# Another start for a one-core layer kernel: the input is turned and scaled by products with diagonals, the first adaLN block is loaded ahead of it, and its sums go to VectorE

## The chip, the cores and the metric

One core of one Trainium2 chip runs the whole program. The metric is the device time of one execution in microseconds. The kernel before has a median of 2390.36 us over three runs (2387.80, 2390.36 and 2390.41 us). About 0.2% (some 4.8 us) is what a measurement of this kernel can tell from no change.

## What is computed

One layer: an adaLN norm, one large projection, a gated convolution beside a chunked gated delta rule, an output projection, a gated feed-forward part and a final adaLN norm. The change touches only the first lines of it.

```python
def adaln(x, gain, shift, scale):
    return rms_norm(x, gain) * (1 + scale[:, None, :]) + shift[:, None, :]
...
    c_act = jax.nn.silu(c)                       # c: [1, 1024]
    mod = c_act @ w_ada[layer] + b_ada[layer]    # w_ada: [1024, 6 * 1024]
    shift_m, scale_m, gate_m, shift_f, scale_f, gate_f = jnp.split(mod, N_MOD, axis=-1)
    h = adaln(x, g_norm_mix[layer], shift_m, scale_m)   # x: [1, 2048, 1024]
    p = h @ w_in[layer]
```

So before the first product with `w_in` can run, three things have to be there for a slice of 128 features: the input's rows divided by their root mean square, turned so that features lie on the partitions; the column of `scale_m` and the column of `shift_m` for these features, each a sum over 1024 products of `c_act` with `w_ada`; and the weights, split into a high and a low part.

## The kernel before

The sequence of 2048 tokens is worked in four blocks of 512 (`NB`, `BLK`), each block as four tiles of 128 tokens (`CH`). The 1024 features are eight slices k of 128 (`KD`). Dense products are made in three parts (`proj`, recorded at L325): high part of the weights times high part of the input, high times low, low times high. `split_w` makes the parts of a 128-column strip of weights: ScalarE casts the high part (`whi`, L368), VectorE subtracts for the low part (`wlo`, L370); the line of `split_w` takes the engine from `lo_engines` if that list holds one, and VectorE if it is empty. It is empty in the front of the kernel before.

The order of the instructions of each engine is fixed while the program is built: a small planner (`Clock`) estimates when each could run, and every engine's instructions are pinned in the order of these estimates. On the chip each engine takes them in that order, and one that waits holds back all behind it on its engine.

The front is what runs before the loop over the blocks. It does this for block 0, in the names of the code:

- **Loads.** SyncE issues `kd` (the first adaLN block, k = 0, from a host array `w_first` that holds it ready for TensorE), two tiles of x, `vt` (k = 1, likewise), two tiles of x, then strips of `w_in` (`wraw`) by turns with the adaLN blocks k = 2, 3 (`yah`, `zs`), and later blocks into `kd`, `vt`, `yah`, `zs` again as they come free. ScalarE issues constants (`ck`, `pc`), the conditioning row `c` sent to all partitions (`gate_m`, in the code `crow`), and `c` as columns (`Gf`, in the code `cs`).
- **Norm.** For each of the four tiles of x (`xt0`, buffers `kq`) ScalarE squares and sums (L482), GpSimd makes the reciprocal root (L476, L477), ScalarE multiplies the tile by it (L759, `x_norm`).
- **Turning.** `transpose_k` (L505) has TensorE turn the four scaled tiles for slice k into one PSUM bank (`pm`).
- **adaLN sums.** `ada_sums(k)` makes the columns of scale and shift. For k = 0 and 1 (`k < AHEAD`) TensorE does it, with sixteen products of one column per k (L776). For k = 2 to 7 VectorE does it with one multiply-and-sum of 128x1024 for each of scale and shift (`sums_of`, L439). ScalarE adds the bias: `Gm` (L782), `Sm` (L783).
- **Scale and split.** `scale_split` (L509, L510, L511): ScalarE applies `Gm` and `Sm` to the turned slice in PSUM, casts the high part `hTh`, VectorE subtracts for the low part `hTl`.
- **Products.** As slice k is ready, TensorE multiplies it with the strips that are there: at step k the strips 0 to k-1 take slice k, and strip k takes slices 0 to k (five strips in all, the fifth in `yal`), and from k = 3 on a small product for the columns a and b (L787, L788). The last slice's dense products belong to the loop behind. L914, a VectorE copy of the a and b columns, is the first instruction of that loop to need the front's last small product.

Of the kernel before, what the change touches and what calls it, by code (L numbers as in the profile page):

```python
# [20 lines left out]
P = 128  # L21
# [20 lines left out]
AHEAD = 2  # L42
# [172 lines left out]
def layer_kernel(ctx, tc, x, c, w_ada, c_col, w_first, cols, g_norm_final, w_in, w_ab, xt, a_log, dt_bias, w_out, w_gate_up,  # L215
# [21 lines left out]
    def misc_ps():  # L237
        return pm.tile([P, 512], F32, name="pm")
# [199 lines left out]
    def sums_of(raw, row, total):  # L438
        nc.vector.scalar_tensor_tensor(raw, raw, 1.0, row, op0=ALU.mult, op1=ALU.mult, accum_out=total)  # L439
# [39 lines left out]
    def sum_squares(t):  # L479
        ss = g0.tile([P, 1], F32, name="ss", bufs=4)  # L480
        junk = sp.tile([P, D], mybir.dt.bfloat16, name="ht", bufs=2)
        nc.scalar.activation(junk, t, AF.Square, accum_out=ss)  # L482
        rms_scale(ss, 1, D)
        return ss
# [182 lines left out]
    with ExitStack() as actx:  # L667
# [82 lines left out]
        def x_load(i):  # L750
            nc.sync.dma_start(xt0[i], x[i * P:(i + 1) * P, :])

        def x_norm():
            ss = []
            for i in range(CH + 1):
                if i < CH:
                    ss.append(sum_squares(xt0[i]))
                if i:
                    nc.scalar.activation(xt0[i - 1], xt0[i - 1], AF.Identity, scale=ss[i - 1])  # L759

        def ada_load(k):
            if k < AHEAD:
                t = ap_.tile([P, 2, KD, P], F32, name=PLACES[k % 4])
                nc.sync.dma_start(t, w_first[k])
            else:
                t = ap_.tile([P, 2, D], F32, name=PLACES[k % 4])
                nc.sync.dma_start(t, w_ada[0:2, k].rearrange("s p n -> p s n"))
            return t

        def ada_sums(k, raw):  # L770
            if k < AHEAD:
                ps = misc_ps()
                sums = [ps[:, s:s + 1] for s in range(2)]
                for s in (1, 0):
                    for i in range(KD):
                        mm(sums[s], raw[:, s, i, :], cs[:, i:i + 1], start=s == 1 and i == 0, stop=i == KD - 1,  # L776
                           skip_group_check=True)
            else:
                sums = [t[:, k:k + 1] for t in totals]
                for s in (1, 0):  # L780
                    sums_of(raw[:, s], crow, sums[s])
            nc.scalar.activation(Gm[:, k:k + 1], sums[1], AF.Identity, scale=col["g_mix"][:, k:k + 1], bias=gb[:, k:k + 1])  # L782
            nc.scalar.activation(Sm[:, k:k + 1], sums[0], AF.Identity, bias=col["b_sm"][:, k:k + 1])  # L783
# [15 lines left out]
        cs = Gf  # L799
        nc.scalar.dma_start(cs, c_col)  # L800
        nc.scalar.activation(cs, cs, AF.Silu)
# [21 lines left out]
        turned = transpose_k(xt0, 0)  # L823
        for k in range(KD):
            ada_sums(k, raws[k])
            ps = turned
            if k + 1 < KD:
                turned = transpose_k(xt0, k + 1)
# [1113 lines left out]
def laid_out(v):  # L1942
# [4 lines left out]
    given["c_col"] = f["c"].reshape(KD, P).T  # L1947
    given["w_first"] = ada[:, :2 * D].reshape(KD, P, 2, KD, P)[:, :, :, :AHEAD].transpose(3, 1, 2, 0, 4)
# [31 lines left out]
```

## Time and profile before

| | |
|---|---|
| median of three runs | 2390.36 us (2387.80 to 2390.41) |
| the profiled execution | 2392.24 us |
| its span | 2390.5 us, so 1.7 us lie around the span |
| TensorE busy (PE) | 2324.8 us, 97% |
| VectorE (DVE), ScalarE (ACT), GpSimd (POOL) busy | 1739.2, 1069.5 and 596.8 us |
| first dense product (L325) | starts at 37.86 us |
| last small product of the front (L788) | starts at 70.86 us |

Rows of the profile are read in this way. PE is TensorE, and PEld its loads of weights, which run beside it. A row of the timeline has a start and a duration in us, the engine, the line of the code, the operation, the tile written and the tiles read, and in brackets how long the engine had stood idle before and whose end released it. Products overlap: the distance from one start to the next is what one costs, not its duration. The granted clock is 1.00 at full speed.

### The profile page before, as it was taken

To read this page: it belongs to the slowest core of one execution; us is meant where nothing else is said; L and a number is where in the kernel's file an instruction comes from. 1 tells how busy PE (TensorE), PEld (TensorE's weight loads), DVE (VectorE), ACT (ScalarE), POOL (GpSimd) and SP (SyncE) were. 2 spreads that over 40 slices of the span, in tenths; PEclk is the share of its full clock that TensorE was granted. 3 is DMA by queue.
4 is the path that set the end of the run, shared out by engine and by line. 5 is a ranking of instruction groups with operands and counts; after the bars stand their busy time and mean duration, and the time that the engine had idled before them with its cause. 6 is when DMAs were issued, how large, how long until landed. Compare 5 with 4: busy or idle time off the path is not lost.

```text
span 2390.5 us, 30803 instructions
## 1 busy us (share of the span) xinstructions
PE 2324.8 (97%) x11167; PEld 1924.3 (81%) x11167; DVE 1739.2 (73%) x2673; ACT 1069.5 (45%) x1865; POOL 596.8 (25%) x651
## 2 busy tenths in 40 slices
PE   6999999999999999999999999999999999999997
PEld 5788778888888888887878888878888887888786
DVE  3788859785978678786665556875655668878887
ACT  4734566445744474366433334433333323322345
POOL 0331444135413461201000000000000035434447
PEclk9999999999999999999999999999999999999999
DMA  7344555534463536255753334763433374333333
GB/s 271 106 139 123 172 177 167 164 98 163 131 209 117 178 111 203 63 167 168 231 187 103 113 89 146 233 185 93 119 97 102 106 252 150 124 106 125 131 132 149
DMA packets 217842, 352.45 MB, mean 147 GB/s; under 512 B 39149, under 2 KB 131609, under 8 KB 217370
## 3 DMA queue, kind: packets, MB, share of 16 engines
q1 hardware_dynamic: 215816, 347.46, 46.2%
q0 software_dynamic: 1152, 2.10, 0.7%
q8 instruction: 87, 1.43, 0.2%
q10 hardware_dynamic: 722, 0.93, 0.1%
q14 instruction: 65, 0.53, 0.1%
HBM read 277.01 MB, written 75.52 MB: 147 GB/s over the span
## 4 chain that ended last, share of the span: by engine, by line
PE 76%; DVE 9%; DMA 6%; ACT 4%; issue 3%; POOL 2%; SPq 0%; ACTq 0%; DVEq 0%; POOLq 0%
PE pd L325 49%; PE pm L325 17%; DVE wlo L370 1%; DVE acc L1814 1%; DMA y<-xT 1%; DVE cv L1231 1%; DMA y<-in_w_ada_dram 1%; POOL wraw L1743 1%; PE pm L898 1%; DMA A12d<-y 1%; PE pm L1113 1%; PE pm L1073 1%; PE pm L1065 1%; PE pm L1179 1%; PE pm L1187 1%
## 5 line engine op out<-in xcount | busy, mean ns | idle before, releaser
L368 ACT CAST whi<-wraw 128x1024 fp32r<-128x1024 f32 x285 | 298.5, 1049 | 368.5 <-PE pd L325 164.2
L370 DVE TENSOR_TENSOR wlo<-wraw,whi 128x1024 fp32r<-128x1024 f32 x285 | 368.4, 1294 | 119.2 <-ACT whi L368 117.5
L325 PE MATMUL pd<-hTh,whi 128*128 128x512 f32 x888 | 363.9, 410 | 6.4 <-DVE edge L1268 3.0
L325 PE MATMUL pd<-hTh,wlo 128*128 128x512 f32 x888 | 349.2, 393 | 0.0
L325 PE MATMUL pd<-hTl,whi 128*128 128x512 f32 x888 | 349.1, 393 | 0.0
L325 PEld LDWEIGHTS pd<-hTh,whi 128*128 128x128 f32 x888 | 168.3, 190 | 40.0 <-issue 3.4
L1608 POOL TENSOR_TENSOR wraw<-wraw 128x1024 f32<-128x1024 f32 x2 | 5.3, 2659 | 781.5 <-DMA wraw<-in_w_down_dram 781.5
L325 PEld LDWEIGHTS pd<-hTh,wlo 128*128 128x128 f32 x888 | 168.1, 189 | 37.1 <-issue 0.2
L325 PEld LDWEIGHTS pd<-hTl,whi 128*128 128x128 f32 x888 | 168.7, 190 | 29.4
L1231 DVE SCALAR_TENSOR_TENSOR cv<-pd,pc,cv 128x511 f32<-128x511 f32 (+2 forms) x173 | 129.1, 746 | 41.7 <-ACT cv L1229 37.9
L1556 DVE TENSOR_TENSOR sg<-sg,pd 128x512 f32<-128x512 f32 x44 | 30.2, 686 | 171.9 <-PE pd L325 171.4
L1814 DVE TENSOR_TENSOR acc<-acc,pd 128x512 f32<-128x512 f32 x192 | 127.4, 679 | 24.7 <-PE pd L325 24.6
L1694 ACT CAST xh<-ra 128x640 fp32r<-128x640 f32 (+1 forms) x85 | 60.4, 721 | 183.8 <-PE pm L325 134.4
L1703 POOL TENSOR_TENSOR xl<-ra,xh 128x640 fp32r<-128x640 f32 (+1 forms) x37 | 62.5, 1688 | 143.9 <-ACT xh L1694 143.1
L1814 DVE TENSOR_TENSOR acc<-acc,pm 128x512 f32<-128x512 f32 x120 | 81.7, 681 | 19.3 <-PE pm L325 18.8
L1743 POOL TENSOR_TENSOR wraw<-wraw 128x512 f32<-128x512 f32 x40 | 69.1, 1750 | 48.7 <-DMA wraw<-in_w_down_dram 41.7
L325 PE MATMUL pd<-whi,ym 128*128 128x512 f32 x256 | 80.4, 390 | 0.0
L325 PE MATMUL pd<-A22h,whi 128*128 128x512 f32 x176 | 70.3, 400 | 6.8 <-DVE sg L1556 6.8
L1313 DVE RECIPROCAL cv<-cv 128x128 f32<-128x128 f32 x64 | 57.1, 926 | 22.3 <-ACT cv L1310 22.2
L325 PE MATMUL pm<-S1h,whi 128*128 128x512 f32 x176 | 69.2, 393 | 1.8 <-ACT whi L368 1.8
L325 PE MATMUL pm<-S1h,wlo 128*128 128x512 f32 x176 | 69.3, 394 | 0.5 <-DVE wlo L370 0.5
L325 PE MATMUL pd<-A22l,whi 128*128 128x512 f32 x176 | 69.8, 396 | 0.0
(450 smaller groups left out, 6195.5 us busy)
## 6 DMA issues: line engine op xcount, KB each, us to landing
wraw<-in_w_in_dram SPq DMA_DIRECT2D x112, 512.0 KB, 4.4
wraw<-in_w_gate_up_dram SPq DMA_DIRECT2D x88, 512.0 KB, 3.7
ra<-act SPq DMA_DIRECT2D x80, 448.0 KB, 3.6
wraw<-in_w_out_dram SPq DMA_DIRECT2D x40, 512.0 KB, 3.7
act<-S SPq DMA_DIRECT2D x80, 256.0 KB, 2.7
act<-act SPq DMA_DIRECT2D x68, 256.0 KB, 2.2
wraw<-in_w_ada_dram SPq DMA_DIRECT2D x32, 512.0 KB, 4.3
cb<-in_x_dram SPq DMA_DIRECT2D x48, 256.0 KB, 3.7
```

The lines of the kernel that those rows point to most:

```text
L325: mm(*args, **kw)
L368: nc.scalar.copy(hi, raw)
L370: (lo_engines.popleft() if lo_engines else nc.vector).tensor_sub(lo, raw, hi.bitcast(F32))
L898: nc.tensor.transpose(ps[:, j * P:(j + 1) * P], src[:, j * P:(j + 1) * P], ident)
L1065: mm(py[:, j * P:(j + 1) * P], Mm[h][:, j, :], T[h][:, j, :], start=True, stop=True)
L1231: nc.vector.scalar_tensor_tensor(cv[:, n - t:], u[:, :BLK - n + t], taps[t], cv[:, n - t:], op0=ALU.mult, op1=ALU.add)
L1313: nc.vector.reciprocal(sy[:, qs], sy[:, qs])
L1556: nc.vector.tensor_add(s5[i], s5[i], a[i])
L1694: nc.scalar.copy(hi, raw[:, c0:c1, :])
L1703: eng.tensor_sub(lo, raw, hi.bitcast(F32))
L1743: nc.gpsimd.tensor_mul(r[:, hs], r[:, hs], gate_f[:, hs])
L1814: nc.vector.tensor_add(accs[s, u][:, ns], accs[s, u][:, ns], ps)
```

## The change

The front's host arrays `w_first` and `c_col` go, and with them the load of `c` as columns. All eight adaLN blocks come from `w_ada` itself, and VectorE makes all sums, k = 0 and 1 too. The tiles of x are no longer multiplied by their scale: GpSimd writes a 128x128 diagonal matrix with the scales of a tile (`diags`, in a buffer of the group `lv`), and TensorE's product of the raw tile's slice with that diagonal turns and scales it at once (`turn_k` takes the place of `transpose_k`). The first adaLN block is issued first, then all four tiles of x, then strips and blocks by turns. Of the low parts, the first strip's is VectorE's as before, those of the next three strips go to GpSimd.

```diff
-        def x_norm():
-            ss = []
-            for i in range(CH + 1):
-                if i < CH:
-                    ss.append(sum_squares(xt0[i]))
-                if i:
-                    nc.scalar.activation(xt0[i - 1], xt0[i - 1], AF.Identity, scale=ss[i - 1])
+        diags = ap_.tile([P, CH, P], F32, name="lv", bufs=NLV)
+
+        def x_scales():
+            for i in range(CH):
+                nc.gpsimd.tensor_scalar_mul(diags[:, i, :], ident, sum_squares(xt0[i]))
+
+        def turn_k(k):
+            ps = misc_ps()
+            for i in range(CH):
+                mm(ps[:, i * P:(i + 1) * P], xt0[i][:, k * P:(k + 1) * P], diags[:, i, :], start=True, stop=True)
+            return ps
...
         def ada_load(k):
-            if k < AHEAD:
-                t = ap_.tile([P, 2, KD, P], F32, name=PLACES[k % 4])
-                nc.sync.dma_start(t, w_first[k])
-            else:
-                t = ap_.tile([P, 2, D], F32, name=PLACES[k % 4])
-                nc.sync.dma_start(t, w_ada[0:2, k].rearrange("s p n -> p s n"))
+            t = ap_.tile([P, 2, D], F32, name=PLACES[k % 4])
+            nc.sync.dma_start(t, w_ada[0:2, k].rearrange("s p n -> p s n"))
             return t
...
         def ada_sums(k, raw):
-            if k < AHEAD:
-                ps = misc_ps()
-                sums = [ps[:, s:s + 1] for s in range(2)]
-                for s in (1, 0):
-                    for i in range(KD):
-                        mm(sums[s], raw[:, s, i, :], cs[:, i:i + 1], start=s == 1 and i == 0, stop=i == KD - 1,
-                           skip_group_check=True)
...
+            sums_of(raw[:, 1], crow, totals[1][:, k:k + 1])
+            sums_of(raw[:, 0], crow, totals[0][:, k:k + 1])
...
         nc.scalar.dma_start(crow, c.to_broadcast([P, D]))
-        cs = Gf
-        nc.scalar.dma_start(cs, c_col)
-        nc.scalar.activation(cs, cs, AF.Silu)
+        nc.scalar.activation(totals[0], epsc.to_broadcast([P, KD]), AF.Silu)
         nc.scalar.activation(crow, crow, AF.Silu)
         nc.scalar.dma_start(c_d, crow[0:1, :])
         raws, strips = [ada_load(0)], []
-        x_load(0)
-        x_load(1)
-        raws.append(ada_load(1))
-        x_load(2)
-        x_load(3)
-        strips.append(next(reqs)[0](w_in, 2048))
-        raws.append(ada_load(2))
-        strips.append(next(reqs)[0](w_in, 2048 + P))
-        raws.append(ada_load(3))
-        strips.append(next(reqs)[0](w_in, 2048 + 2 * P))
-        x_norm()
+        for i in range(CH):
+            x_load(i)
+        x_scales()
+        lo_engines.extend((nc.vector, nc.gpsimd, nc.gpsimd, nc.gpsimd))
+        for k in range(3):
+            strips.append(next(reqs)[0](w_in, 2048 + k * P))
+            raws.append(ada_load(k + 1))
```

The extra activation of 8 columns (`totals[0]` from `epsc`) only has ScalarE load its table of Silu before the row `c` is there; its result is overwritten.

What stands where, first on TensorE. Before, from the program's first product on (`ck,kq` is a turn by the identity, `Gf,kd` and `Gf,vt` are the sums for k = 0 and 1, `hTh,whi` the first dense product):

```order
L505 MATMUL pm<-ck,kq 128x128
L776 MATMUL pm<-Gf,kd 128x1 x16
L505 MATMUL pm<-ck,kq 128x128
L776 MATMUL pm<-Gf,vt 128x1 x12
L505 MATMUL pm<-ck,kq 128x128 x2
L776 MATMUL pm<-Gf,vt 128x1 x4
L505 MATMUL pm<-ck,kq 128x128 x12
L325 MATMUL pd<-hTh,whi 128x512 x2
```

In the changed kernel, at the same place (`lv,kq` is a product of a raw tile's slice with a diagonal):

```order
L761 MATMUL pm<-lv,kq 128x128 x16
L324 MATMUL pd<-hTh,whi 128x512
L324 MATMUL pd<-hTl,whi 128x512
L324 MATMUL pd<-hTh,wlo 128x512
L761 MATMUL pm<-lv,kq 128x128 x4
L324 MATMUL pd<-hTh,whi 128x512
L324 MATMUL pd<-hTl,whi 128x512
L324 MATMUL pd<-hTh,wlo 128x512
```

The 32 products with one column are gone, and four slices (sixteen products) are turned ahead of the first dense one. Second, VectorE. Before, its first instruction on `w_in` or `w_ada` is the low part of strip 0 (`wlo`), and sums (`ms`) stand there from k = 2 on:

```order
L370 TENSOR_TENSOR wlo<-wraw,whi 128x1024
L439 SCALAR_TENSOR_TENSOR yah,ms<-yah,gate_m 128x1024 x2
L511 TENSOR_TENSOR hTl<-pm,hTh 128x512
L370 TENSOR_TENSOR wlo<-wraw,whi 128x1024
L511 TENSOR_TENSOR hTl<-pm,hTh 128x512 x2
L439 SCALAR_TENSOR_TENSOR zs,ms<-zs,gate_m 128x1024 x2
L370 TENSOR_TENSOR wlo<-wraw,whi 128x1024
L511 TENSOR_TENSOR hTl<-pm,hTh 128x512
```

In the changed kernel:

```order
L438 SCALAR_TENSOR_TENSOR kd,ms<-kd,gate_m 128x1024 x2
L369 TENSOR_TENSOR wlo<-wraw,whi 128x1024
L510 TENSOR_TENSOR hTl<-pm,hTh 128x512
L438 SCALAR_TENSOR_TENSOR vt,ms<-vt,gate_m 128x1024 x2
L510 TENSOR_TENSOR hTl<-pm,hTh 128x512
L438 SCALAR_TENSOR_TENSOR yah,ms<-yah,gate_m 128x1024 x2
L510 TENSOR_TENSOR hTl<-pm,hTh 128x512
L438 SCALAR_TENSOR_TENSOR zs,ms<-zs,gate_m 128x1024 x2
```

The sums of k = 0 open the row, each later slice's two sums stand behind the low part of the slice before it, and only one low part of a strip is left between them. Third, ScalarE, from its Silu of the row `c` on. Before:

```order
L802 ACTIVATE gate_m<-gate_m 128x1024
L801 ACTIVATE Gf<-Gf 128x8
L482 ACTIVATE ht,ss<-kq 128x1024
L803 DMA c_d<-gate_m 1x1024
L482 ACTIVATE ht,ss<-kq 128x1024
L759 ACTIVATE kq<-kq,ss 128x1024 x2
L782 ACTIVATE Gm<-pm,gb,pc 128x1
L783 ACTIVATE Sm<-pm,pc 128x1
L482 ACTIVATE ht,ss<-kq 128x1024
L782 ACTIVATE Gm<-pm,gb,pc 128x1
```

In the changed kernel:

```order
L791 ACTIVATE gate_m<-gate_m 128x1024
L792 DMA c_d<-gate_m 1x1024
L481 ACTIVATE ht,ss<-kq 128x1024
L772 ACTIVATE Gm<-ms,gb,pc 128x1
L481 ACTIVATE ht,ss<-kq 128x1024
L774 ACTIVATE Sm<-ms,pc 128x1
L481 ACTIVATE ht,ss<-kq 128x1024 x2
L367 CAST whi<-wraw 128x1024
L508 ACTIVATE pm<-pm,Sm,Gm 128x512
L509 CAST hTh<-pm 128x512
```

The wait for the sums of TensorE (`Gm<-pm`) between the squares of the second and the third tile is gone, and so are the four multiplications of tiles. Behind the front, from the copy of L914 on, the instructions of every engine stand in the same order in both kernels.

More of the change, by code (lines that the diff above doesn't have):

```diff
@@ L214, in layer_kernel @@
 @with_exitstack
-def layer_kernel(ctx, tc, x, c, w_ada, c_col, w_first, cols, g_norm_final, w_in, w_ab, xt, a_log, dt_bias, w_out, w_gate_up,
+def layer_kernel(ctx, tc, x, c, w_ada, cols, g_norm_final, w_in, w_ab, xt, a_log, dt_bias, w_out, w_gate_up,
                  w_down, cst, out):
@@ L782, in ada_sums @@
-            nc.scalar.activation(Gm[:, k:k + 1], sums[1], AF.Identity, scale=col["g_mix"][:, k:k + 1], bias=gb[:, k:k + 1])
-            nc.scalar.activation(Sm[:, k:k + 1], sums[0], AF.Identity, bias=col["b_sm"][:, k:k + 1])
+            sums_of(raw[:, 1], crow, totals[1][:, k:k + 1])
+            sums_of(raw[:, 0], crow, totals[0][:, k:k + 1])
+            nc.scalar.activation(Gm[:, k:k + 1], totals[1][:, k:k + 1], AF.Identity,
+                                 scale=col["g_mix"][:, k:k + 1], bias=gb[:, k:k + 1])
@@ L822, in layer_kernel @@
         clock.kept.add(ps_ab.name)
-        turned = transpose_k(xt0, 0)
+        turned = turn_k( 0)
         for k in range(KD):
@@ L827, in layer_kernel @@
             if k + 1 < KD:
-                turned = transpose_k(xt0, k + 1)
+                turned = turn_k( k + 1)
             scale_split(ps, k, Gm, Sm, *hT)
```

8 lines of the change are left out of this document (1 added, 7 removed).

## The prediction

> **What bounds the kernel now.** I read the busy times of three stretches first, cut at the first dense product (37.86 us), at the end of the front (71.28, where L914 starts) and at 100 us. The columns are length, then busy time and count for PE, PEld, DVE, ACT and POOL, granted clock, DMA share, GB/s.
>
> ```profile
> 0.00:37.86 37.86, 17.79 (x81) 16.19 (x81) 4.22 (x11) 14.91 (x24) 3.83 (x15) 1.00 0.82 304
> 37.86:71.28 33.42, 32.79 (x138) 24.78 (x139) 21.79 (x32) 17.61 (x34) 1.11 (x2) 1.00 0.41 141
> 71.28:100.00 28.72, 24.37 (x104) 19.25 (x103) 26.71 (x56) 21.55 (x42) 10.87 (x13) 0.94 0.47 147
> ```
>
> In the first stretch no engine is half busy, and VectorE works 4.22 us; from 37.86 on TensorE is full; behind 71.28 VectorE is. So the front is a wait of 37.86 us and then 33 us of products. The chain of waits (start, length, what) says of what the wait is made:
>
> ```profile
> 2.14 10.70 DMA Gf<-in_c_col_dram
> ...
> 15.14 1.07 ACT kq L759
> ...
> 16.73 6.62 PE pm L776 x32
> ...
> 23.67 4.91 PE pm L776 x24
> ...
> 29.11 1.51 PE pm L776 x8
> ...
> 71.02 0.23 PE pm L788
> ```
>
> The load of c as columns holds ScalarE to 12.86 us. Then the sums for k = 0 and 1 take 6.62 + 4.91 + 1.51 = 13.0 us of the chain on TensorE (the program's 16 products for k = 0 are 32 records, 0.41 us each product), and ScalarE's squares of the last two tiles stand behind them. All of that is what the change takes out. TensorE's last small product of the front ends at 71.1.
>
> **The change, step by step.** I follow the new order and put the trace's durations on it, up to the same last small product.
>
> *Step 1, the row c.* VectorE's first sum and ScalarE's squares now both start behind the Silu of the row.
>
> ```profile
> 10.40 1.06 ACT L802 ACTIVATE gate_m<-gate_m 128x1024 f32<-128x1024 f32 x1 [6.09 <-DMA gate_m<-in_c_dram]
> ...
> 12.97 1.04 ACT L482 ACTIVATE ht<-kq 128x1024 bf16<-128x1024 f32 x1
> ...
> 13.92 0.19 ACT L482 ACTIVATION_READ_ACCUMULATOR ht<-kq 128x1 f32 x1
> 14.01 1.04 ACT L482 ACTIVATE ht<-kq 128x1024 bf16<-128x1024 f32 x1
> 14.20 0.19 POOL L476 TENSOR_SCALAR ss<-ss 128x1 f32<-128x1 f32 x1 [12.79 <-ACT ht L482]
> 14.47 0.56 POOL L477 TENSOR_TENSOR ss<-ss,mhalf 128x1 f32<-128x1 f32 x1
> ```
>
> The row landed at 10.40. The early loads by queue (window 0 to 15 us):
>
> ```profile
> DMA packets 1485, 5.05 MB, mean 336 GB/s; under 512 B 288, under 2 KB 544, under 8 KB 1229
> ...
> q10 hardware_dynamic: 576, 0.67, 13.4%
> ```
>
> 1485 - 1229 = 256 packets of 8 KB are the two blocks of `w_first`; ScalarE's queue (q10) has its few packets among them. The new first block is two rows of 4 KB for each partition. If the queues take turns by packets, the row passes fewer bytes and lands up to 1.4 us earlier; if by bytes, at 10.40 again. I take 9.4, ends 9.0 and 10.4. The last tile of x lands at 11.5 or so by my estimate (3.64 MB at the 0.41 MB/us that the 13 us after a start of 2.6 show: 5.05 MB in 12.4 us), before ScalarE needs it. Silu then ends at 10.45.
>
> *Step 2, squares.* Four at 14.01 - 12.97 = 1.04 us, with `Gm` and `Sm` between (0.39 and 0.29, below): the first reaches GpSimd at 11.6, the last at 15.4. GpSimd needs 0.83 for a scale (14.20 to 15.03), and a diagonal more. That operation, a column times 128x128, is not in the trace. The nearest rows:
>
> ```profile
> L930 POOL TENSOR_SCALAR nexpa<-nexpa 128x4 f32<-128x4 f32 x1 | 0.2, 243 | 23.0 <-ACT nexpa L929 23.0
> ...
> L1125 POOL TENSOR_TENSOR lv<-ym,ck 128x512 f32<-128x512 f32 x16 | 16.4, 1041 | 0.3
> ...
> L1608 POOL TENSOR_TENSOR wraw<-wraw 128x1024 f32<-128x1024 f32 x2 | 5.3, 2659 | 781.5 <-DMA wraw<-in_w_down_dram 781.5
> ```
>
> Between 0.24 and 1.04, I take 0.45: a quarter of the way in columns. With 0.1 us of gaps a tile is 1.4 us of GpSimd, so it, not ScalarE, paces: diagonals at 13.0, 14.4, 15.8 and 17.3.
>
> *Step 3, turning.* A product with a diagonal is an fp32 product and not a turn:
>
> ```profile
> 115.54 1.16 PE pm L995 x8
> ...
> 117.39 0.44 PE pm L898 x4
> ...
> 123.55 0.89 PE pm L1113 x8
> ```
>
> Four fp32 products of 128x128 (eight records) cost 0.89 to 1.16 at full rate, where four turns (L898 in the same chain) cost 0.44. At the start TensorE runs at half rate: dense products (L325) start every 0.42 us at first, every 0.23 later, though the granted clock reads 1.00.
>
> ```profile
> 39.28 0.80 PE L325 MATMUL pd<-hTh,whi 128*128 128x512 f32 x1 [0.63 <-ACT whi L368]
> ...
> 39.88 0.63 PE L325 MATMUL pd<-hTl,whi 128*128 128x512 f32 x1
> 40.30 0.63 PE L325 MATMUL pd<-hTh,wlo 128*128 128x512 f32 x1
> ...
> 44.36 0.43 PE L325 MATMUL pd<-hTh,wlo 128*128 128x512 f32 x1
> 44.63 0.39 PE L325 MATMUL pd<-hTh,whi 128*128 128x512 f32 x1
> 44.86 0.40 PE L325 MATMUL pd<-hTl,whi 128*128 128x512 f32 x1
> ```
>
> So 0.45 for each. Behind the third diagonal stand six products (2.7 us from 15.9: 18.6), then the last of k = 0 (19.05, 19.3 with its write). ScalarE's scale and cast take 1.4, and the first dense product starts at **20.7, where it was 37.86**. Strip 0's `whi` and `wlo` are done by then: its load is the next 0.5 MB behind x, ScalarE casts it behind the last square, VectorE subtracts by 18.
>
> *Step 4, the pace of slices.* VectorE is in order: `hTl` of a slice, two sums for the next, then ScalarE's `Sm`, scale and cast, then `hTl` again. The trace has this loop:
>
> ```profile
> 45.99 0.69 DVE L511 TENSOR_TENSOR hTl<-pm,hTh 128x512 fp32r<-128x512 f32 x1 [0.63 <-ACT hTh L510]
> ...
> 46.60 1.22 DVE L439 SCALAR_TENSOR_TENSOR kd<-kd,gate_m 128x1024 f32<-128x1024 f32 x1
> ...
> 47.74 1.22 DVE L439 SCALAR_TENSOR_TENSOR kd<-kd,gate_m 128x1024 f32<-128x1024 f32 x1
> 47.86 0.39 ACT L782 ACTIVATE Gm<-ms,gb,pc 128x1 f32<-128x1 f32 x1 [1.90 <-DVE kd L439]
> ...
> 48.15 1.03 ACT L368 CAST whi<-wraw 128x1024 fp32r<-128x1024 f32 x1
> ...
> 49.09 0.29 ACT L783 ACTIVATE Sm<-ms,pc 128x1 f32<-128x1 f32 x1
> ...
> 50.81 0.69 DVE L511 TENSOR_TENSOR hTl<-pm,hTh 128x512 fp32r<-128x512 f32 x1 [0.37 <-ACT hTh L510]
> ```
>
> 50.81 - 45.99 = 4.8 us. Slice 1 is there at 25.5. For slice 2, strip 2 also is needed, whose cast stands behind `Gm`: 25.5, `hTl` 0.65, one sum 1.14, `Gm` 0.39, cast 1.03: 28.7. Then GpSimd's low part, twice L1125's width: 2 x 1.04 = 2.05 us if alone, 2.66 by L1608. TensorE waits for it until **30.8**. VectorE is meanwhile off the two-operand sums, which end as the cast does.
>
> *Step 5, products.* From 30.8 TensorE has work without a gap: of the 105 dense products up to the last small one 14 are done, 91 x 0.23 = 20.9; 16 small ones (0.23, the last row of the chain) 3.7; slices 5, 6 and 7 to turn, 3 x 1.0 = 3.0 (slice 4 is turned in an earlier gap); and half rate again for its first 5.1 us (39.28 to 44.36 above), 12 products x 0.2 = 2.4. Sum 30.0: the front ends at 60.8 instead of 71.1. By the same count the front before is 105 x 0.23 + 3.7 + 22 turns x 0.11 + 2.4 + idle 0.6 = 33.3 from 37.86, which gives 71.2: the count holds. From 30.8 on later slices come in time: VectorE's sums for slices 3 to 7 at 2.3 each, the fifth strip's low part and the `hTl` between them end near 48, and the last slices wait for their turning, which is TensorE's own.
>
> *What hides the rest.*
>
> ```profile
> 34.18 1.23 DVE L370 TENSOR_TENSOR wlo<-wraw,whi 128x1024 fp32r<-128x1024 f32 x1 [26.48 <-ACT whi L368]
> ```
>
> VectorE's four sums added, 4 x 1.14, lie where it stood idle 26.48 us. Three low parts of 1.23 leave VectorE. Behind L914 nothing is reordered on any engine, and its loads are issued as buffers come free, so earlier too. What is late next is the same as before: VectorE, 26.71 of 28.72 us busy. I count the shift at full length.
>
> **Sum:** 71.1 - 60.8 = 10.3 us. The profiled execution took 2392.24, which gives 2381.9; the median lies 1.9 below it, so **2380.1 us**.
>
> **Rivals.**
>
> *TensorE is already at full rate.*
>
> ```profile
> 32.24 1.11 PE L505 MATMUL pm<-ck,kq 128*128 128x128 f32 x4 [0.35 <-ACT kq L759]
> ```
>
> The products with diagonals, some 16 from 13 to 20 us, may do what the one-column products did not (four turns behind 13 us of those still took 1.11 us, against L898's 0.44). Then 2.4 us more: 2377.7. The pieces of work between 21 and 31 are short, against it. The Trainium skill (TensorE: Matmul & The Clock Gate, Part 1) has a window of about 3.4 us of sustained work for the full clock, and an idle one for its loss. By that rule the run of products before 20 us could suffice, which gives this time; the 5.1 us above agree with a window that need not begin with the work.
>
> *GpSimd and VectorE block each other.* Beside a sum, GpSimd's subtraction of 128x64 took 0.87 us, from 42.27 to 43.14, though one of 128x512 takes 1.04:
>
> ```profile
> 41.74 1.22 DVE L439 SCALAR_TENSOR_TENSOR zs<-zs,gate_m 128x1024 f32<-128x1024 f32 x1
> ...
> 42.27 0.87 POOL L820 TENSOR_TENSOR wabs<-wab,wabs 128x64 fp32r<-128x64 f32 x1 [8.14 <-ACT wabs L819]
> ```
>
> If each of the three low parts gets ahead of a sum instead of behind it, the loop of step 4 is 2.05 longer three times: 6.2 of the 10.3 us go, 2386.3. It decides by tenths, since the cast ends as the second sum does. The Trainium skill (SBUF — State Buffer, Terms) says that the two share a port pair, held for a whole instruction, and that the loser fully blocks; that rule speaks against this change and would give this time, and the row of 0.87 agrees with it.
>
> *Slower: TensorE stays at half rate through the front.* Its gaps at 21 to 31 us, between pieces of 1 to 2 us, keep it so, and the 107 products behind cost 0.2 more each. It decides at 63 of them (2.4 + 10.3 = 12.7 us); for all 107 and the turns it is 24.4 instead of 2.4: 2402. Against it: before, 5.1 us of dense work were enough, and from 30.8 there is no gap.
>
> *The start doesn't come forward so far.* The row c or x lands only when all early loads have, near 13.5, and a stall behind the front does not move with it: within 0.2%, near 2387. The order behind the front speaks against it.
>
> **Chances.** Forecast 0.70 (its own range 2377.7 to 2383.5: c -0.4 to +1.0, the diagonal -0.8 to +2.4, the low parts up to +1.2), full rate 0.13, port 0.07, no shift 0.06, slower 0.04. The runs differ by 2.6 us. The range 2376 to 2385 holds the first two and part of the third. Faster by over 0.2% (4.8 us): 0.70 + 0.13 + half the port's 0.07, 0.87; within 0.09; slower 0.04.
>
> **What would show it.** First dense product near 20.7; a loop of 4.8 us from `hTl` to `hTl`; low parts on POOL of 2.05 us behind, not among, the sums; dense starts 0.23 apart by 36; L914's line (L899 there) near 61; and the stretch behind it as long as before. Wrong if the row lands after 11, if starts stay 0.42 apart, or if that stretch grows.

## The result, and the profile after

The changed kernel takes 2377.43 us (median of six runs, 2373.47 to 2380.77), beside 2389.86 us for the kernel before in the same session (six runs): a ratio of 0.9947, with a 95% interval of 0.9932 to 0.9961. A second comparison gave 2378.45 against 2389.48, 0.9960 (0.9946 to 0.9973). So it is 11 to 12 us faster, where 10.3 were forecast. The sum came out well, but two of its terms did not, and they err in opposite directions: that it came so close is in part luck.

The stretches of the changed kernel, cut at the same two events as before (columns as in the prediction; the copy is L899 here):

```profile
0.00:24.79 24.79, 7.48 (x33) 6.70 (x33) 4.32 (x11) 9.55 (x16) 7.69 (x19) 1.00 0.94 366
24.79:62.93 38.14, 34.29 (x154) 26.05 (x155) 22.89 (x37) 19.32 (x37) 9.02 (x5) 0.96 0.54 187
```

The wait ahead of the first dense product went from 37.86 to 24.79 us: 13.07 us gained. The products behind it went from 33.42 to 38.14 us: 4.72 given back. The front ends **8.35 us earlier** (copy at 62.93 instead of 71.28), not 10.3. The profiled execution took 2373.47 us, with a span of 2371.7, and is 18.8 shorter than the one of before; so 10.4 us of that difference came behind the front, where every engine has the same order of instructions. The two traces lie further apart than the medians: the one of the changed kernel is the fastest of its six runs, and the one of before (2392.24 us) is slower than that kernel's median. Both parts are followed below.

The timeline of the changed kernel, first ScalarE and GpSimd, then VectorE, then TensorE:

```profile
10.84 1.06 ACT L791 ACTIVATE gate_m<-gate_m 128x1024 f32<-128x1024 f32 x1 [7.13 <-DMA gate_m<-in_c_dram]
11.93 0.48 ACTq L792 DMA_DIRECT2D c_d<-gate_m  x1
12.46 1.06 ACT L481 ACTIVATE ht<-kq 128x1024 bf16<-128x1024 f32 x1 [0.56 <-ACT gate_m L791]
...
13.70 0.66 POOL L475 TENSOR_SCALAR ss<-ss 128x1 f32<-128x1 f32 x1 [12.30 <-ACT ht L481]
14.44 0.56 POOL L476 TENSOR_TENSOR ss<-ss,mhalf 128x1 f32<-128x1 f32 x1
15.10 0.62 POOL L756 TENSOR_SCALAR lv<-ck,ss 128x128 f32<-128x128 f32 x1
...
18.39 1.47 POOL L756 TENSOR_SCALAR lv<-ck,ss 128x128 f32<-128x128 f32 x1
...
20.89 0.61 POOL L756 TENSOR_SCALAR lv<-ck,ss 128x128 f32<-128x128 f32 x1
28.04 2.35 POOL L369 TENSOR_TENSOR wlo<-wraw,whi 128x1024 fp32r<-128x1024 f32 x1 [6.54 <-ACT whi L367]
32.91 2.37 POOL L369 TENSOR_TENSOR wlo<-wraw,whi 128x1024 fp32r<-128x1024 f32 x1 [2.52 <-ACT whi L367]
...
40.65 2.82 POOL L369 TENSOR_TENSOR wlo<-wraw,whi 128x1024 fp32r<-128x1024 f32 x1 [4.12 <-ACT whi L367]
...
18.16 1.23 DVE L369 TENSOR_TENSOR wlo<-wraw,whi 128x1024 fp32r<-128x1024 f32 x1 [3.85 <-ACT whi L367]
24.77 0.69 DVE L510 TENSOR_TENSOR hTl<-pm,hTh 128x512 fp32r<-128x512 f32 x1 [5.39 <-ACT hTh L509]
...
29.59 0.69 DVE L510 TENSOR_TENSOR hTl<-pm,hTh 128x512 fp32r<-128x512 f32 x1 [1.84 <-ACT hTh L509]
...
34.46 0.69 DVE L510 TENSOR_TENSOR hTl<-pm,hTh 128x512 fp32r<-128x512 f32 x1 [1.84 <-ACT hTh L509]
...
24.79 0.49 PE L324 MATMUL pd<-hTh,whi 128*128 128x512 f32 x1 [0.70 <-ACT hTh L509]
25.51 0.50 PE L324 MATMUL pd<-hTl,whi 128*128 128x512 f32 x1 [0.23 <-DVE hTl L510]
25.85 0.40 PE L324 MATMUL pd<-hTh,wlo 128*128 128x512 f32 x1
26.08 1.05 PE L761 MATMUL pm<-lv,kq 128*128 128x128 f32 x8
...
30.44 0.80 PE L324 MATMUL pd<-hTh,wlo 128*128 128x512 f32 x1 [1.69 <-POOL wlo L369]
...
33.17 0.63 PE L324 MATMUL pd<-hTh,wlo 128*128 128x512 f32 x1
33.59 0.46 PE L324 MATMUL pd<-hTh,whi 128*128 128x512 f32 x1
33.88 0.39 PE L324 MATMUL pd<-hTl,whi 128*128 128x512 f32 x1
35.33 0.50 PE L324 MATMUL pd<-hTh,wlo 128*128 128x512 f32 x1 [1.05 <-POOL wlo L369]
```

The reader is to see three delays. The row c lands at 10.84 and the first square starts only at 12.46, since the issue of the row's copy to memory (`c_d`, at 11.93, for 0.48 us) stands between. The third diagonal takes 1.47 us instead of 0.62: it begins at 18.39, while VectorE's subtraction of 18.16 runs until 19.39. And TensorE waits twice for a low part made by GpSimd, 1.69 and 1.05 us.

### The profile page after: what moved, and what is told of

It is laid out like the page before. It is cut to its first block, busy times and chain, and to the rows that moved or that the text cites. A ratio compares the mean times of both kernels' runs of the same rounds, so it can differ in the third digit from the quotient of the medians.

```text
span 2371.7 us, 30754 instructions
## 1 busy us (share of the span) xinstructions
PE 2309.1 (97%) x11135; PEld 1911.4 (81%) x11135; DVE 1743.0 (73%) x2678; ACT 1066.2 (45%) x1861; POOL 611.1 (26%) x658
## 3 DMA queue, kind: packets, MB, share of 16 engines
q8 instruction: 87, 1.43, 0.2%
## 4 chain that ended last, share of the span: by engine, by line
PE 71%; DVE 10%; DMA 6%; ACT 5%; issue 4%; POOL 3%; SPq 0%; DVEq 0%; POOLq 0%; ACTq 0%
PE pd L324 46%; PE pm L324 18%; DVE acc L1799 2%; DVE wlo L369 1%; DMA y<-xT 1%; DMA cb<-in_x_dram 1%; DVE cv L1216 1%; ACT whi L367 1%; ACT L1254 1%; POOL cv L1380 1%; DMA A12d<-y 1%; PE pm L1058 1%; PE pm L1050 1%; PE pm L1164 1%; DVE xl L1688 1%
## 5 line engine op out<-in xcount | busy, mean ns | idle before, releaser
L324 PE MATMUL pd<-S2h,whi 128*128 128x512 f32 x176 | 68.6, 390 | 0.9 <-ACT whi L367 0.9
```

The costliest lines, as they stand in the source:

```text
L324: mm(*args, **kw)
```

## The experiments

Twelve experiments follow; the first two are the two kernels as they are. "First" is the start of the first dense product, "copy" the start of VectorE's copy of a and b at the front's end, "behind" the rest of the span; all three are from one profiled run, in us. The median and the ratio are over all runs of a kernel, the ratio against the kernel before on the same chip. The rows come from several chips, so ratios compare better than medians.

| kernel | median | ratio (95%) | first | copy | behind |
|---|---|---|---|---|---|
| before | 2389.86 | | 37.86 | 71.28 | 2319.2 |
| before, another run | 2384.75 (one run) | | 38.17 | 70.98 | 2312.0 |
| changed | 2377.43 | 0.9947 (0.9932, 0.9961) | 24.79 | 62.93 | 2308.8 |
| changed, again | 2378.45 | 0.9960 (0.9946, 0.9973) | 24.62 | 62.77 | 2314.1 |
| changed, without diagonals | 2377.02 | 0.9957 (0.9940, 0.9974) | 24.98 | 59.00 | 2311.3 |
| before, with diagonals | 2393.44 | 1.0023 (1.0010, 1.0035) | 40.27 | 74.24 | 2316.5 |
| low parts on VectorE | 2376.98 | 0.9950 (0.9936, 0.9963) | 24.55 | 62.54 | 2313.0 |
| diagonals by VectorE | 2375.43 | 0.9942 (0.9929, 0.9956) | 21.42 | 60.91 | 2310.3 |
| row c first | 2373.21 | 0.9937 (0.9920, 0.9954) | 21.13 | 59.28 | 2309.0 |
| row c first, without diagonals | 2379.95 | 0.9961 (0.9947, 0.9975) | 22.49 | 58.54 | 2323.2 |
| x ahead | 2373.92 | 0.9939 (0.9921, 0.9956) | 23.27 | 62.04 | 2310.3 |
| three edits | 2368.89 | 0.9918 (0.9904, 0.9933) | 20.63 | 58.83 | 2309.2 |
| four edits | 2366.99 | 0.9911 (0.9897, 0.9926) | 17.79 | 56.14 | 2307.9 |
| four edits, turns in place of diagonals | 2372.36 | 0.9925 (0.9907, 0.9944) | 20.16 | 53.30 | 2320.3 |

### Both kernels again

The changed kernel and the kernel before, as they are.

> The changed kernel once more. Theory: the front gives 8.35 us and nothing else is lasting; so the VectorE copy of the a and b columns (L899) starts at 62.9 us again, within 0.3, while the stretch behind it, 2308.8 us in the first profile of this kernel, comes out longer (about 2313 to 2318), with another number of half-rate windows than the four of the first profile. Over five rounds 8 to 12 us are saved. Rival: the change has a lasting effect behind the front too; then that stretch is 2309 us again, with the same windows at the same places, and 15 to 19 us are saved.

> The kernel before once more, for a second profile. Theory: L914 starts at 71.3 us again, within 0.3; the stretch behind it, 2319.2 us in the first profile, moves by several us with the number of half-rate windows (seven in the first profile). Rival: the stretch behind the front and its windows are the same in every run of one kernel, 2319 us.

The fronts repeat to 0.3 us (62.77 and 70.98). The spans do not: 2376.8 instead of 2371.7, and 2383.0 instead of 2390.5. The kernel before ran from 2379.79 to 2394.19 us in the 20 runs of this comparison. What varies lies behind the front (2314.1 us instead of 2308.8, and 2312.0 instead of 2319.2), so both theories held.

### Which part of the change carries the gain

Without the diagonals, all else as changed: ScalarE multiplies the tiles and TensorE turns them by the identity, as before.

```diff
-                nc.gpsimd.tensor_scalar_mul(diags[:, i, :], ident, sum_squares(xt0[i]))
...
+                    nc.scalar.activation(xt0[i - 1], xt0[i - 1], AF.Identity, scale=ss[i - 1])
...
-            for i in range(CH):
-                mm(ps[:, i * P:(i + 1) * P], xt0[i][:, k * P:(k + 1) * P], diags[:, i, :], start=True, stop=True)
...
+            return transpose_k(xt0, k)
```

> The changed kernel, but the tiles of x are multiplied by their scales on ScalarE and turned by the identity, as before; loads, sums on VectorE and low parts on GpSimd as changed. Theory: the sums carry the gain and the diagonals do not; first dense product at 25 to 27 us, the copy of the a and b columns at 61 to 63 us (62.9 with diagonals), saved as much as by the whole change or 1 to 2 us more. Rival: the diagonals carry it, since they take four multiplications from ScalarE; then the copy comes at 67 us or later and most of the gain is gone.

The stretches of this kernel:

```profile
0.00:24.98 24.98, 4.40 (x16) 2.86 (x16) 6.69 (x15) 15.03 (x23) 5.41 (x16) 1.00 0.95 363
24.98:59.00 34.02, 32.58 (x138) 24.44 (x139) 21.49 (x34) 18.05 (x35) 7.80 (x5) 1.00 0.58 210
```

The first dense product starts no later without the diagonals (24.98 against 24.79), and the products behind it take 34.02 instead of 38.14 us. So the rest of the change (sums by VectorE, no load of c as columns, the order of loads) brings the copy forward by 71.28 - 59.00 = 12.3 us, 2 us beyond the theory's range, and the diagonals take back 3.9. No run takes the three parts of that rest apart from one another. The median hides the difference (2377.02); what the traces say of that comes last.

Not all of the 3.9 us is the products' own cost. Of the 4.12 us by which the second stretches differ, TensorE's busy time (34.29 against 32.58) makes 1.7, and waits make the other 2.4. VectorE's timeline without the diagonals shows why:

```profile
16.77 1.23 DVE L438 SCALAR_TENSOR_TENSOR vt<-vt,gate_m 128x1024 f32<-128x1024 f32 x1 [2.56 <-DMA vt<-in_w_ada_dram]
...
24.96 0.69 DVE L510 TENSOR_TENSOR hTl<-pm,hTh 128x512 fp32r<-128x512 f32 x1 [0.33 <-ACT hTh L509]
...
27.91 0.68 DVE L510 TENSOR_TENSOR hTl<-pm,hTh 128x512 fp32r<-128x512 f32 x1
```

The planner now puts a sum of slice 1 (`vt`) ahead of the first low part, and slice 1 is there 2.95 us behind slice 0, instead of 4.82. So this run prices the diagonals together with the order that comes with them.

The other way round, the kernel before with nothing but the diagonals:

```diff
-                    nc.scalar.activation(xt0[i - 1], xt0[i - 1], AF.Identity, scale=ss[i - 1])
...
+                nc.gpsimd.tensor_scalar_mul(diags[:, i, :], ident, sum_squares(xt0[i]))
...
-        turned = transpose_k(xt0, 0)
+        turned = turn_k(0)
...
-                turned = transpose_k(xt0, k + 1)
+                turned = turn_k(k + 1)
```

> The kernel before with the diagonals alone: loads, sums of slices 0 and 1 on TensorE and low parts on VectorE stay as before. Theory: nothing is gained; the sums on TensorE still stand in front, and fp32 products with a diagonal cost two records where a turn by the identity costs one: the copy at 72 to 75 us (71.3 before), 0 to 4 us lost. Rival: the diagonals carry the gain; copy at 66 us or earlier.

The timeline of TensorE in this kernel:

```profile
26.77 4.62 PE L780 MATMUL pm<-Gf,vt 128*128 128x1 f32 x21
31.25 2.06 PE L762 MATMUL pm<-lv,kq 128*128 128x128 f32 x8
34.66 2.08 PE L762 MATMUL pm<-lv,kq 128*128 128x128 f32 x8 [1.36 <-POOL lv L757]
37.38 2.08 PE L762 MATMUL pm<-lv,kq 128*128 128x128 f32 x8 [0.65 <-POOL lv L757]
40.27 0.80 PE L325 MATMUL pd<-hTh,whi 128*128 128x512 f32 x1 [0.80 <-ACT hTh L510]
```

The sums still hold TensorE, and it waits for diagonals behind them. The copy comes 3.0 us later, and the median is 1.0023 of before: slower, measured. The two runs agree on the price of the diagonals, 3 to 4 us of the front, but not on its place: here 2.4 of the 3.0 us lie ahead of the first dense product (40.27 against 37.86), there none.

### What the work on GpSimd costs

All low parts back on VectorE:

```diff
-        lo_engines.extend((nc.vector, nc.gpsimd, nc.gpsimd, nc.gpsimd))
```

> The changed kernel with all low parts of strips on VectorE. In the changed kernel TensorE waited 1.69 and 1.05 us for GpSimd's low parts of strips 1 and 2 (2.35 us each), while VectorE stood idle 1.84 us in each loop. Theory: the part given to GpSimd costs time; on VectorE it takes 1.2 us inside that idle time, the loop stays 4.8 to 4.9 us, and the copy of the a and b columns starts at 61.3 to 62.2 us (62.9 in the changed kernel). Rival: the low parts lengthen VectorE's loop by 1.2 us three times; then the copy comes at 64 us or later.

The copy moves by 0.39 us only (62.54), short of the theory's range. TensorE's waits for low parts of 1.69 and 1.05 us shrink to one of 0.53, but the loop of the slices stays at 4.82 us (`hTl` at 24.53 and 29.35). But this front has two half-rate windows, one behind the other (29.75 to 36.58, by the trace's record of the clock), where the changed kernel has one, so the run does not price the low parts alone. As the kernels stand, this part of the change costs little and brings nothing.

The diagonals by VectorE in place of GpSimd:

```diff
-                nc.gpsimd.tensor_scalar_mul(diags[:, i, :], ident, sum_squares(xt0[i]))
+                nc.vector.tensor_scalar_mul(diags[:, i, :], ident, sum_squares(xt0[i]))
```

> The changed kernel with the four diagonals written by VectorE. Theory: GpSimd's chain of scale and diagonal, 1.65 us for each tile and 1.47 us for the third diagonal beside VectorE's low part, sets the start; without the diagonals the scales are done at 18.1 instead of 20.8 us, the first dense product starts at 21.5 to 23 us (24.8 in the changed kernel) and the copy at 60 to 61.5 us (62.9). Rival: sixteen products at half rate set the start whoever writes the diagonals; then the first dense product stays at 24.3 us or later.

VectorE's timeline in this kernel:

```profile
14.84 0.29 DVE L756 TENSOR_SCALAR lv<-ck,ss 128x128 f32<-128x128 f32 x1 [0.71 <-POOL ss L476]
...
17.96 0.29 DVE L756 TENSOR_SCALAR lv<-ck,ss 128x128 f32<-128x128 f32 x1 [0.75 <-POOL ss L476]
18.16 1.22 DVE L369 TENSOR_TENSOR wlo<-wraw,whi 128x1024 fp32r<-128x1024 f32 x1
```

A diagonal takes 0.29 us there, the last is done at 18.25 instead of 21.50, and one comes every 1.04 us: ScalarE's squares set the pace, not GpSimd. The first dense product comes 3.4 us earlier, the copy 2.0 (60.91), as the theory had it.

### What sets the start

The row c as the first load on ScalarE's queue; the two constants behind it, and VectorE's `gb`, which needs one of them, too:

```diff
-    nc.scalar.dma_start(ck[:, :P], cst[:, :P])
...
-    nc.scalar.dma_start(pc, cols)
...
-    nc.vector.scalar_tensor_tensor(gb, col["b_cm"], 1.0, col["g_mix"], op0=ALU.add, op1=ALU.mult)
...
         nc.scalar.dma_start(crow, c.to_broadcast([P, D]))
+        nc.scalar.dma_start(ck[:, :P], cst[:, :P])
+        nc.scalar.dma_start(pc, cols)
+        nc.vector.scalar_tensor_tensor(gb, col["b_cm"], 1.0, col["g_mix"], op0=ALU.add, op1=ALU.mult)
```

> The changed kernel with the row c as the first load of ScalarE's queue, ahead of the two constants. Theory: ScalarE's queue takes turns with SyncE's, and the row waits there for the constants ahead of it; first in its queue it lands at 7 to 9 us (10.8 in the changed kernel), and the first dense product and the copy of the a and b columns come 1.5 to 3 us earlier: copy at 60 to 61.4 us. Rival: all early loads share the bandwidth and the row lands at 10 us or later wherever it stands; copy at 62.5 to 63 us.

ScalarE's timeline in this kernel:

```profile
6.38 1.06 ACT L791 ACTIVATE gate_m<-gate_m 128x1024 f32<-128x1024 f32 x1 [2.72 <-DMA gate_m<-in_c_dram]
...
9.37 1.06 ACT L478 ACTIVATE ht<-kq 128x1024 bf16<-128x1024 f32 x1 [1.94 <-DMA kq<-in_x_dram]
```

The row lands at 6.38 instead of 10.84, earlier than expected, and the next wait takes its place: the first square now waits 1.94 us for x. The copy comes at 59.28, 3.65 us earlier, which is more than the theory gave. The place of a load in its queue was worth about as much as the diagonals cost.

The same edit without the diagonals:

> The kernel without diagonals and with the row c as the first load of ScalarE's queue. Theory: both savings add; the copy at 56.5 to 58 us (59.0 without diagonals alone, 71.3 before), 13 to 15 us saved in the front. Rival: the turning waits for x and not for the row; copy at 58.7 to 59.2 us.

The first dense product comes 2.5 us earlier than without the edit (22.49 against 24.98; ScalarE waits 1.79 us for x here too), the copy at 58.54 only 0.46: by the trace's record of the clock TensorE came to full rate at 31.5 us, 9.0 behind the first dense product, where it was 4.8 (29.8). Neither range held: the copy lies 0.16 us ahead of the rival's, but its reason, the wait for x, is only a part, since the first dense product did come earlier.

The tiles of x loaded ahead of the first adaLN block, the row c left where it is:

```diff
-        raws, strips = [ada_load(0)], []
         for i in range(CH):
             x_load(i)
+        raws, strips = [ada_load(0)], []
```

> The changed kernel with one edit: the four tiles of x are loaded ahead of the first adaLN block instead of behind it. Theory (ScalarE's squares wait for the row c at 10.8 us, so it does not matter which of the two comes first): first dense product 24.3 to 25.2, copy 62.5 to 63.3, median 2376 to 2380. Rival A (the order of the loads itself carries part of the gain): copy 64.5 or later. Rival B (the row's landing depends on what SyncE's queue holds): copy 61.5 or earlier.

None of the three ranges held. The row landed at 9.69, 1.15 earlier, and ScalarE fitted one square in ahead of it; the copy came at 62.04, 0.9 earlier. So the order of these loads matters, less than the row's own place.

### Together

Three edits: the row c first, the diagonals by VectorE, all low parts on VectorE.

> The changed kernel with three edits together: the row c first on ScalarE's queue, the diagonals written by VectorE, all low parts of strips on VectorE. Theory (the three waits lie one behind the other on the way to the first dense product, so their gains add up: 3.65 us for the row, 2.0 for the diagonals, 0.4 for the low parts, of the copy at 62.93): first dense product 17.8 to 18.5 us, copy of the a and b columns 56 to 57.5, median 2369 to 2374. Rival (the loads of x and of the first strip come next): ScalarE's squares or the cast of the first strip wait for a load, first dense product 19.5 or later, copy 58.5 or later, median 2373 to 2378.

ScalarE's timeline in this kernel:

```profile
9.47 1.06 ACT L478 ACTIVATE ht<-kq 128x1024 bf16<-128x1024 f32 x1 [1.75 <-DMA kq<-in_x_dram]
...
11.20 0.39 ACT L769 ACTIVATE Gm<-ms,gb,pc 128x1 f32<-128x1 f32 x1 [0.57 <-DVE kd L435]
12.34 0.29 ACT L771 ACTIVATE Sm<-ms,pc 128x1 f32<-128x1 f32 x1 [0.76 <-DVE kd L435]
```

The gains do not add up. With the row there at 6.67, ScalarE waits 1.75 us for x, then 0.57 and 0.76 us for VectorE's sums, ahead of the other squares; the copy at 58.83 is only 0.45 better than with the row alone. The rival was right on the front, though it named the loads alone; the median (2368.89) lies below both ranges, and what it gained beyond the front is not explained.

Four edits, the fourth being x ahead of the first adaLN block:

> As the kernel with three edits, and the four tiles of x are loaded ahead of the first adaLN block. Theory (with the row first, the first square waits for x, as it did for 1.94 us with the row alone moved): the squares start near 7.5 to 8, first dense product 16 to 17, copy 54 to 55.5, median 2367 to 2373. Rival (VectorE's first sum then waits for the adaLN block, or ScalarE for the first strip, landing near 16): copy within 0.7 us of that of the kernel with three edits.

VectorE's and TensorE's timeline:

```profile
9.88 0.17 DVE L789 SCALAR_TENSOR_TENSOR gb<-pc 128x8 f32<-128x8 f32 x1 [8.56 <-DMA pc<-in_cols_dram]
...
13.55 1.23 DVE L435 SCALAR_TENSOR_TENSOR kd<-kd,gate_m 128x1024 f32<-128x1024 f32 x1
...
16.17 1.22 DVE L366 TENSOR_TENSOR wlo<-wraw,whi 128x1024 fp32r<-128x1024 f32 x1 [0.24 <-ACT whi L364]
...
17.79 0.50 PE L324 MATMUL pd<-hTh,whi 128*128 128x512 f32 x1 [2.02 <-ACT hTh L506]
```

The squares start at 7.73 as expected, but VectorE is in order: its first diagonal stands behind `gb`, which waits for a constant until 9.88, and the sums stand behind the diagonals, until 16.0. The copy at 56.14 is 2.7 better than with three edits, but 0.6 us later than the theory's range, and so is the first dense product (17.79, expected at 16 to 17). The median of 2366.99, 0.9911 of before (0.9897 to 0.9926), is the best of all kernels.

The same, with ScalarE's multiplications and turns in place of the diagonals:

> As the kernel with four edits (row c first, all low parts on VectorE, x ahead of the first adaLN block), but with ScalarE's four multiplications and turns by the identity in place of the diagonals. Theory (products with diagonals are a cost in every arrangement, since each turned slice takes TensorE 0.89 us instead of 0.44): ScalarE works without a gap from 7.7 to some 17 us, first dense product 18.5 to 19.5, one to two microseconds later than with diagonals, copy all the same 53 to 55.5, ahead of 56.14. Rival (with the row early the squares and multiplications of ScalarE, 8.4 us together, set the start, and the diagonals are worth their price there): copy 56.2 or later.

The front is the shortest of all (copy at 53.30, as the theory had it; the first dense product is 0.7 us later than that): here too the diagonals cost more, 2.84 us, than they bring. Yet the whole kernel does not gain by it: 0.9925 of before against 0.9911, with intervals that overlap, and in the profiled runs the stretch behind the copy is 12.4 us longer (the profiled run is this kernel's slowest, and the fastest of the one with four edits).

## Why the prediction was right in sum and wrong in two terms

| step | predicted | measured |
|---|---|---|
| 1: row c lands | 9.4 | 10.84 |
| 2: first diagonal done | 13.0 | 15.72 |
| 2: last diagonal done | 17.3 | 21.50 |
| 3: first dense product | 20.7 | 24.79 |
| 4: from `hTl` to `hTl` | 4.8 | 4.82, 4.87 |
| 4: TensorE's last wait for a low part ends | 30.8 | 35.33 |
| 5: from there to the last small product's end | 30.0 | 27.4 (62.73) |

**Step 1 fell.** The row did not pass its rivals' packets; it landed near the bound of 10.4 and beyond. That it is the row that counts is shown (row c first: 3.65 us); why it landed where it did is not, and the earlier landings at 6.2 to 6.8 came with its place ahead of the constants. The prediction calls the packets of ScalarE's queue few, but its own line has 576 of 1485. Its 3.64 MB up to the last tile of x is a slip of units too (3.81 in those of the 5.05 MB, so 11.9 instead of 11.5 us); nothing hung on that.

**Step 2 was mis-sized.** The first diagonal is 2.7 late: 1.44 by the row, 0.56 by the issue of `c_d`, which stood in the quoted order but was not priced, 0.47 by GpSimd's first operation (0.66 instead of 0.19) and 0.17 by the diagonal itself (0.62 instead of 0.45). The following three come every 1.65 us, not 1.43, and one of them 0.85 later still. The last fits the blocking of the second rival, met at another place than the one given: the Trainium skill (SBUF — State Buffer, Terms) has GpSimd and VectorE share a port pair that is held for a whole instruction, and the 1.47 beside VectorE's subtraction, and the 2.82 of the third low part beside a sum, agree with it. Without the diagonals it also went the other way: a sum of VectorE that starts at 25.57, while GpSimd's low part runs from 24.52 to 26.90, takes 2.41 us instead of 1.22.

**Steps 3 and 4 held as a mechanism:** the loop took 4.8 us, and TensorE did wait for the low part. GpSimd took 2.35 us for it, between the 2.05 and the 2.66 given, and the three low parts did not hold up the loop.

**Step 5: the 2.4 us for half rate were not paid at that place.** TensorE was at full rate at 24.8 already (25.51, 25.85, 26.08: 0.34 apart and then 0.23), which is what the first rival, with a chance of 0.13, had named. It lost it in the waits up to 30.44, ran at half rate until 33.6 (33.17 to 33.59: 0.42), and then waited for the next low part. So the half rate lay in the shadow of a wait. 91 dense products at 0.227, 16 small ones and three turned slices at 0.89 are 27 us, as measured.

In the front, then, TensorE was let go 4.5 us later than predicted and needed 2.6 less from there: 8.35 us instead of 10.3.

**"Behind L914 the shift counts at full length" was the other wrong term.** The medians moved by 12.4 us, 4 more than the front. The order there is unchanged, but the granted clock is not. The stretch behind the same wait of TensorE, 14 us behind the copy, in three kernels; first the kernel before (the product that ends the wait, then the stretch of 3.41 us):

```profile
85.29 0.66 PE L325 MATMUL pd<-hTh,whi 128*128 128x512 f32 x1 [3.02 <-DVE edge L1268]
...
85.41:88.82 3.41, 3.41 (x9) 2.64 (x10) 3.34 (x4) 1.62 (x4) 2.64 (x2) 0.50 0.43 105
```

The changed kernel:

```profile
76.93 0.47 PE L324 MATMUL pd<-hTh,whi 128*128 128x512 f32 x1 [3.00 <-DVE edge L1253]
...
78.10:81.50 3.40, 3.40 (x9) 2.62 (x9) 3.33 (x7) 0.99 (x4) 1.59 (x1) 0.50 0.51 125
```

The kernel with four edits:

```profile
70.13 0.47 PE L324 MATMUL pd<-hTh,whi 128*128 128x512 f32 x1 [3.01 <-DVE edge L1252]
...
70.13:73.54 3.41, 3.41 (x15) 2.82 (x16) 3.34 (x4) 1.75 (x4) 2.77 (x2) 1.00 0.31 114
```

The wait is the same, 3.0 us. Before, the granted clock is 0.50 as soon as it ends, and TensorE makes 9 products in 3.41 us; in the changed kernel it falls 1.1 us later, at 78.07; with four edits it does not fall at all, and 15 products are made. The clock goes by a grid of its own: within one run, all half-rate windows start a whole multiple of 3.413 us apart (before: 85.41, 283.38, 317.51, 1092.34, 1225.46, 1573.62 and 2256.28 are 0, 58, 68, 295, 334, 436 and 636 steps from the first). The Trainium skill (TensorE: Matmul & The Clock Gate, Part 1) says that this window is free-running, 3413 ns; the runs agree. Before, one step of this grid holds nearly all of the wait (82.00 to 85.41, TensorE busy for 0.39 us of it); in the changed kernel the step from 74.66 to 78.07 holds 2.27 us of it (busy for 1.14); with four edits the grid cuts the wait at 68.33, and the two steps keep 2.20 and 1.62 us of work. So where a wait falls in the grid decides whether it costs a window. All profiled runs, by the distance of the grid's first point behind the copy (us), with the number of half-rate windows behind it (the last 30 us left out) and the time behind it:

```
row c first, without diagonals   0.28   6   2323.2
four edits, turned               0.33   7   2320.3
before                           0.47   7   2319.2
before, with diagonals           0.51   5   2316.5
low parts on VectorE             1.34   3   2313.0
row c first                      1.49   3   2309.0
changed                          1.49   3   2308.8
changed, without diagonals       1.49   2   2311.3
changed, again                   1.56   4   2314.1
three edits                      1.58   3   2309.2
x ahead                          1.61   4   2310.3
diagonals by VectorE             1.93   1   2310.3
four edits                       1.95   1   2307.9
before, another run              3.19   4   2312.0
```

From 0.3 to 0.5 there are five to seven windows and 2316 to 2323 us; from 1.3 to 2.0 one to four, and 2308 to 2314. A front may bring its own distance: TensorE works from a point of the grid (where full rate begins) to the copy, so that the distance would be what this stretch leaves over. That is not shown: of the two kernels with two profiles, the changed one repeats (1.49 and 1.56), but the two runs of before have 0.47 and 3.19, and their spans differ by 7.5 us.

This accounts for about half: in the kernel before, a window costs TensorE the time of 6 products of 0.227 us, 1.4 us, and the profiled runs differ by four windows, some 5.5 of the 10.4 us. TensorE's busy time agrees: from the copy on it is 2274.23 of 2318.72 us before (71.28 to 2390) and 2267.36 of 2308.07 in the changed kernel (62.93 to 2371), so 6.9 us less work and 3.8 less waiting; why the waits are shorter is open. The windows also fit two of the three kernels with turns, whose medians run against their fronts (six and seven windows). The third, the changed kernel without diagonals, has two windows in its profile, which is its fastest run, so for its median this is not shown. It is all read from one profile of each kernel, or two, and no run sets the grid: that the 4 us of the medians beyond the front are all of this kind is likely but not shown. What the experiments do show is the front's 8.35 us: 12.3 gained, less the 3.9 that came with the diagonals.

## What to carry to other kernels

When a wait at the start of a kernel is taken out, price each instruction that now stands between the first landing and the first product, the issue of a store and the place of a load in its queue too: moving one small load ahead of two constants was worth 3.65 us here, about what the diagonals cost. Then take a change apart: the sums on VectorE and the loads (together; they were not parted) carried this one, while the product with a diagonal, which saves ScalarE four multiplications, cost TensorE twice the time of a turn on every slice. And in a kernel that TensorE bounds, compare parts by an event at their end, and not by the median alone: here the diagonals' 3 to 4 us at the front's end were lost in differences of several us behind it, of which the clock's half-rate windows are a part.

## What had not been expected of the hardware

Which products bring TensorE to full rate. Sixteen products with diagonals ahead of the first dense one were enough in the changed kernel (25.85 to 26.08, above: 0.23), where they fill a whole step of the grid (20.05 to 23.46, busy for 3.41 us). In the kernel before with diagonals, where the last of the sixteen came with waits of 1.36 and 0.65 us (above) and no step is filled from 30.37 to 40.61 (busy for 2.93, 2.08 and 2.42 us), they were not: its dense products start 0.42 apart at first (42.01, 42.44). Sixteen turns by the identity were not enough either; they are less work (4.5 us of TensorE against 7.5) and come in four pieces, so no run tells whether it is their kind or their gaps. The products with one column filled steps without that effect (kernel before, 17.14 to 23.96: busy throughout; four turns at 32.24 still took 1.11 us). TensorE in the kernel with four edits and turns:

```profile
17.19 1.12 PE L501 MATMUL pm<-ck,kq 128*128 128x128 f32 x4 [1.46 <-ACT kq L755]
...
21.91 0.63 PE L324 MATMUL pd<-hTh,whi 128*128 128x512 f32 x1
22.33 0.63 PE L324 MATMUL pd<-hTl,whi 128*128 128x512 f32 x1
```

They are 0.42 us apart, five products into the dense work. And waits that are each far shorter than the window of 3.41 us can lose the full rate again, when they fall into one step of the grid. The changed kernel:

```profile
26.88:30.29 3.41, 0.99 (x5) 0.36 (x3) 1.57 (x4) 2.61 (x5) 2.25 (x1) 1.00 0.48 123
30.29:33.70 3.41, 3.26 (x8) 2.59 (x9) 2.33 (x4) 2.15 (x4) 0.89 (x2) 0.50 0.96 393
```

The first step holds a wait of 0.88 us and most of the one of 1.69: 2.42 us without work, and the next is at half rate. Over the 14 profiled runs, once full rate was reached and up to the last 30 us, a full-rate step with less than 1.39 us of idle time was never followed by one at half rate, and one with more than 1.88 always was. Between the two both occur: 1.39 us lost the rate with three edits (22.86 to 26.28), 1.87 did not in the other run of before (313.10 to 316.51).
